# Moving the power tables of a state-space stage into PSUM, and reordering the stage

## The chip, the cores and the metric

The kernel runs on one core of a Trainium2 chip. The metric is device time in microseconds (us) for one launch; lower is better. Names of the engines: PE is TensorE (matmuls and transposes), DVE is VectorE, ACT is ScalarE, POOL is GpSimd, SP is SyncE, which here only issues DMAs.

## The reference

A block of eight stages on a sequence of 256 tokens of width 1024. The change touches the first stage only, a diagonal state-space mixer ("S5") with 64 groups of 16 channels and 64 complex states a group. Cut to what matters:

```python
def s5_mixer(x, a_re, a_im, log_dt, b_re, b_im, c_re, c_im, d_skip, w_glu, w_out):
    u = x.astype(f32).reshape(bsz, seq, SSM_GROUPS, SSM_GROUP)
    ...
    lbar_re = mag * jnp.cos(lam_im * dt)
    lbar_im = mag * jnp.sin(lam_im * dt)
    ...
    bu_re = jnp.einsum('blgh,gph->lbgp', u, bb_re)
    bu_im = jnp.einsum('blgh,gph->lbgp', u, bb_im)
    ...
    _, _, s_re, s_im = lax.associative_scan(
        _ssm_combine, (a_seq_re, a_seq_im, bu_re, bu_im), axis=0)
    y = (jnp.einsum('lbgp,ghp->blgh', s_re, c_re.astype(f32))
         - jnp.einsum('lbgp,ghp->blgh', s_im, c_im.astype(f32)))
    y = y.reshape(bsz, seq, D_MODEL) + d_skip.astype(f32) * x.astype(f32)
    h = jax.nn.gelu(y).astype(x.dtype)
    val, gate = jnp.split(h @ w_glu, 2, axis=-1)
    z = val * jax.nn.sigmoid(gate)
    return (z @ w_out).astype(x.dtype)
```

Seven stages of matmuls (gated feed-forwards, attention, a hybrid layer) follow. They are the same in both kernels.

## The kernel before

`s5_states` computes y and its gelu, `main_stream` all that follows. The tokens are cut into 32 blocks of 8. Inside a block the answer is a sum over lags; between blocks the states are carried by a tree over the 32 blocks. The 64 groups are handled in pairs: 32 pairs lie along the free axis, the 2 x 64 states of a pair on the 128 partitions.

The start (up to line 362) computes lambda and its powers `LR` = lambda^8 ... lambda^1 (real and imaginary part), and `LRs`, `LRd`, their sum and difference, in SBUF. A complex product is made of three real ones with these tables. The tables of B and C are transposed by PE to PSUM and copied by ACT to SBUF (`nBr`, `nBi`, `Cc`).

After that each piece of work is a named step, put on a fixed engine, and each engine runs its steps in the order of the string `ORDER`. The order of DVE, PE, ACT and POOL is thus written out by hand; only waits on data and on buffers move it. The steps, with lines, are these (the first digit is a part i, a half f or a channel tile ch):

- `cp`, `cs`: C times a coefficient (POOL, line 460) and its sums (DVE, lines 464 to 466).
- `vp`, `vt`, `vs`: 24 products B x power of 128x512 elements (DVE, line 470), four transposes of each (PE, line 500), the copy to SBUF (ACT, line 504). A product has six buffers, a transposed one two PSUM buffers (`pv`).
- `sm`, `sp`, `sd`, `st`, `ss`: block states by matmul (line 512), the copy of the shared third product (ACT, line 515), the sum (DVE, line 518), a transpose (line 524), the copy (ACT, line 535).
- `wp`, `wq`: 24 products C x power of 128x448 elements (POOL, line 470) and their sums (DVE for i = 0 to 5, POOL for 6 and 7; line 481).
- `bp`: powers of lambda for the tree (DVE, lines 542 to 551). `mg`, `bo`: the tree up and down for the halves f = 0 and 1 (DVE; each is a complex multiply-add of two products and two sums, lines 559 to 562).
- `lp`, `lc`, `lb`, `ld`, `lm`, `ls`: lag matrices (PE, line 606), their block diagonal (POOL at line 618, or ACT), the D term on lag 0 (POOL, lines 626 and 627), the matmuls over lags (PE, line 634, two PSUM buffers `py`), the copy out.
- `ms`, `om`, `os`, `ot`, `oa`, `og`, `oh`, `ol`: the states before each block, masked (ACT, line 588), times C (PE, line 653), copied, transposed (line 665), summed (line 669), gelu, and split in a high and a low half for the next stage.
- `wd`, `wh`, `wl`: the first weights of the next stage, loaded and split (line 705). Their raw buffer is one of four; loads of more weights wait on SP until one is free.

Line 470 stands for both DVE and POOL products, since both go through the helper `times`.

Of the kernel before, what the change touches and what calls it, by code (L numbers as in the profile page):

```python
# [166 lines left out]
vp71 xt10 cp10 bd01 cp11 xt01 xs10 vp10 vt71 cp00 cs1 ug1 vt10 wp61 vp72 ut1 wp01 vs10 cp01 vt72 wp21 vs71 vp42 vp12  # L167
us1 wp31 vp11 vt12 wp71 vp02 wp41 vs72 ut5 vt11 vp70 cs2 vp41 vs12 ut7 us5 vp00 vt70 vs11 vp50 wr1 sm1 vs70 wp11 wp72
vt00 vp32 us7 vp51 vt02 sp1 sm7 ug0 ut6 vs02 sd1 vp01 vs00 st1 vp52 vt50 ut2 us6 sp7 wp51 vs50 vt51 us2 vp31 vt52 vt32
vs51 bd00 vs52 ss1 sd7 wr0 wp12 ut0 vt01 vs01 vp61 sm5 vt31 cs0 vp30 st7 us0 ut4 sp5 dt xs01 ss7 sm0 vp22 sd5 wp52  # L170
wp42 vs32 vt22 vp40 vs31 vp21 vt40 ds wp40 wp00 wp30 bd11 vp20 vs22 wp22 us4 st5 vt30 xt00 sp0 bd10 wp32 vs30 xs00
wp02 sd0 ut3 st0 vt20 wq31 wq40 xt11 wq00 ss0 wp10 us3 sm3 vs20 wq01 wq10 ss5 wq11 vt21 vs21 wp20 vs40 lp1 wq21 vt61
wq41 sp3 bp0 xs11 sd3 sm2 st3 vt42 sp2 vp62 vs61 lp0 lb11 sd2 wp70 lc0 ss3 wq70 bp1 vp60 st2 lp4 vt62 vs42 ss2 lc4
wq20 vt60 wq71 lb10 vs60 lb00 mg00 ld1 lp7 mg01 lp2 lc2 vt41 lm1 vs62 sm6 lb40 bp2 ld0 mg02 vs41 ls1 sm4 ld4 lb20 sp6
bp3 wq30 bo00 sd6 wp50 lb70 sp4 lm0 lb71 sd4 lp3 lb31 ld2 st6 bo01 lm4 ls0 bo02 ss6 lb30 bo03 ls4 st4 ld7 lm7 ss4 ls7
wq51 bo04 bo05 wp62 ld3 ms01 wq50 ms00 mg10 mg11 wp60 lm3 wq60 lm2 wq61 lp6 lc6 mg12 wd lp5 lb51 ls2 lb60 lb50 bo10
bo11 ld5 om01 om00 bo12 ld6 os01 lm5 os00 bo13 ls3 ot1 bo14 bo15 ot3 lm6 ms11 oa1 ot2 ls5 oa3 om11 og1 ms10 oa2 og3
oh31 oh10 og2 wh1 os11 ol31 wh0 oh30 om10 ls6 oh21 ot0 ol10 oh20 ol21 oh11 os10 ol20 ol11 ol30 wl1 oa0 og0 ot4 wl0
oh00 ot6 oh01 oa4 og4 oa6 ot5 og6 ol01 ol00 ot7 oh41 ol41 oh61 ol61 oa7 oh60 oa5 og7 oh40 oh71 oh70 og5 ol40 ol60 ol70
ol71 oh51 oh50 ol51 ol50  # L180
# [3 lines left out]
def s5_states(nc, tc, a, V, S, G, T, const, raws, ats, mm_ps, tp_ps, xts, ident, h, **_):  # L184
    """y = SSM(x) + d * x, then gelu; returns the transposed halves [P, NK, SEQ] of it, and the next stage's
    first weights, split."""
# [26 lines left out]
    with tc.manual_schedule(engines=PAP):  # L213
# [111 lines left out]
        Cc = buf("c", [P, 2, NGP, SH])
        for k, raw in enumerate(c_raw):
            S.copy(Cc[:, k], transposed(lambda hh: raw[:, hh, :], py_ps))
        S.activation(out=sm([P, 1], "warm"), in_=Cc[:, 1, 0, 0:1], func=AF.Gelu_apprx_tanh)
# [208 lines left out]
        # states at the borders of the blocks, by a tree  # L537
        def border_power(lv):
            """lambda^(TC 2^lv)"""
            lr, li = sm([P, 2, NGP], f"Lr{lv}"), sm([P, 2, NGP], f"Li{lv}")  # L540
            if lv == 0:
                V.tensor_copy(lr[:, 0], LR[:, 0, 0, :])
                V.tensor_copy(li[:, 1], LR[:, 0, 1, :])
            else:
# [3 lines left out]
                V.tensor_sub(lr[:, 0], x1, d2)
                V.scalar_tensor_tensor(li[:, 1], pr, 2.0, pi, op0=ALU.mult, op1=ALU.mult)
            V.tensor_copy(lr[:, 1], lr[:, 0])  # L550
            V.tensor_scalar(li[:, 0], li[:, 1], -1.0, None, op0=ALU.mult)
            Lr.append(lr)
            Li.append(li)
# [977 lines left out]
```

## Time and profile before

| | us |
|---|---|
| median of 3 runs | 1397.32 |
| lowest and highest of them | 1396.32, 1399.21 |
| span of the profiled execution | 1397.1 |
| of it: from the start to the first matmul of the next stage | 114.0 |

Busy time over the whole span: PE 1353.8 us (97%), DVE 940.1 (67%), ACT 699.6 (50%), POOL 117.4 (8%). The profiled execution is the time from the first to the last instruction of one run. Shares over the whole span describe the seven matmul stages; the stage that the change touches is 8% of it, so it has to be read in windows of its own. In rows of the timeline the columns are start, duration, engine, line, operation, out<-in, shapes and count; merged rows give the duration of all their instructions together, and successive instructions of one engine overlap by some hundredths of a us.

### The profile page before, as it was taken

How to read it: one execution, taken by the hardware profiler on the slowest of the kernel's cores; microseconds unless marked ns; L12 is line 12 of the kernel's file. 1: busy time of each engine (PE TensorE's matmuls, PEld its weight loads, DVE VectorE, ACT ScalarE, POOL GpSimd, SP SyncE). 2: the span in 40 equal slices, each digit the busy share in tenths (PEclk: the TensorE clock that was granted, in tenths of full speed). 3: DMA queues.
4: the chain of work that ended last, by engine and by line, in shares of the span. 5: the costliest groups of instructions: out<-in, count | busy, mean ns of one | idle time of the engine just before them, and what ended most of it. 6: DMA issues, size and time to landing. Idle time of an engine off the chain costs nothing.

```text
span 1397.1 us, 20195 instructions
## 1 busy us (share of the span) xinstructions
PE 1353.8 (97%) x7192; PEld 1116.3 (80%) x7192; DVE 940.1 (67%) x1936; ACT 699.6 (50%) x1114; POOL 117.4 (8%) x178
## 2 busy tenths in 40 slices
PE   6879999999999999999999999999999999999998
PEld 5677878888788878888777888888888788888887
DVE  8896675555776875555788567564668956756463
ACT  3536544444577644444455545454554554545351
POOL 7650000000011100000110000000001000000000
PEclk8899999999999999999999999999999999999999
DMA  5005857555564366565455455564654545655561
GB/s 122 1 2 195 256 169 234 182 181 181 165 211 137 91 195 197 182 194 189 126 175 177 146 181 181 181 210 152 213 169 133 171 145 167 195 181 187 175 200 56
DMA packets 141285, 230.72 MB, mean 165 GB/s; under 512 B 15096, under 2 KB 83776, under 8 KB 141120
## 3 DMA queue, kind: packets, MB, share of 16 engines
q1 hardware_dynamic: 141184, 229.43, 52.3%
q8 instruction: 56, 0.92, 0.3%
q14 instruction: 45, 0.37, 0.1%
HBM read 228.35 MB, written 1.05 MB: 164 GB/s over the span
## 4 chain that ended last, share of the span: by engine, by line
PE 86%; DVE 8%; DMA 2%; issue 1%; ACT 1%; SPq 1%; POOL 0%; ACTq 0%; POOLq 0%; DVEq 0%
PE acc L807 8%; PE acc L808 8%; PE acc L806 8%; PE mm_ffn_g_t L807 6%; PE mm_ffn_g_t L808 6%; PE mm_ffn_g_t L806 6%; PE mm_ff_g_t L806 4%; PE mm_ff_g_t L808 4%; PE mm_ff_g_t L807 4%; PE tp L865 2%; PE mm_hy_t L806 2%; PE mm_hy_t L807 2%; PE mm_hy_t L808 2%; PE mm_hy_b_t L808 1%; PE mm_hy_b_t L806 1%
## 5 line engine op out<-in xcount | busy, mean ns | idle before, releaser
L769 DVE TENSOR_TENSOR wl<-raw,wh 128x512 fp32r<-128x512 f32 (+1 forms) x834 | 542.7, 684 | 159.8 <-ACT wh L763 143.7
L763 ACT CAST wh<-raw 128x1024 fp32r<-128x1024 f32 (+1 forms) x417 | 436.6, 1048 | 260.7 <-DMA raw<-in_ffn_w_gu_dram 41.1
L806 PE MATMUL acc<-wh,bTh 128*128 128x512 f32 x544 | 213.3, 392 | 0.0
L807 PE MATMUL acc<-wh,bTl 128*128 128x512 f32 x544 | 212.1, 390 | 0.5 <-DVE bTl L852 0.2
L808 PE MATMUL acc<-wl,bTh 128*128 128x512 f32 x544 | 212.1, 390 | 0.0
L806 PE MATMUL mm_ffn_g_t<-wh,xTh 128*128 128x512 f32 x352 | 141.2, 401 | 2.1 <-ACT xTh L851 2.1
L807 PE MATMUL mm_ffn_g_t<-wh,xTl 128*128 128x512 f32 x352 | 138.3, 393 | 0.5 <-DVE xTl L852 0.5
L808 PE MATMUL mm_ffn_g_t<-wl,xTh 128*128 128x512 f32 x352 | 138.0, 392 | 0.0
L852 DVE TENSOR_TENSOR bTl<-tp,bTh 128x256 fp32r<-128x256 f32 (+1 forms) x104 | 52.6, 512 | 122.8 <-ACT bTh L851 122.8
L807 PEld LDWEIGHTS acc<-wh,bTl 128*128 128x128 f32 x544 | 102.2, 188 | 22.6 <-DVE bTl L852 2.0
L808 PEld LDWEIGHTS acc<-wl,bTh 128*128 128x128 f32 x544 | 102.1, 188 | 21.3
L806 PEld LDWEIGHTS acc<-wh,bTh 128*128 128x128 f32 x544 | 102.1, 188 | 21.1 <-ACT bTh L851 0.3
L851 ACT CAST bTh<-tp 128x256 fp32r<-128x256 f32 (+1 forms) x104 | 45.2, 443 | 144.7 <-PE tp L865 131.0
L806 PE MATMUL mm_ff_g_t<-wh,xTh 128*128 128x512 f32 x256 | 102.6, 401 | 0.0
L808 PE MATMUL mm_ff_g_t<-wl,xTh 128*128 128x512 f32 x256 | 99.9, 390 | 0.0
L807 PE MATMUL mm_ff_g_t<-wh,xTl 128*128 128x512 f32 x256 | 99.7, 389 | 0.0
L806 PEld LDWEIGHTS mm_ffn_g_t<-wh,xTh 128*128 128x128 f32 x352 | 66.4, 189 | 15.2 <-ACT xTh L851 2.5
L808 PEld LDWEIGHTS mm_ffn_g_t<-wl,xTh 128*128 128x128 f32 x352 | 66.5, 189 | 14.0
L807 PEld LDWEIGHTS mm_ffn_g_t<-wh,xTl 128*128 128x128 f32 x352 | 66.6, 189 | 13.9 <-DVE xTl L852 1.1
L806 PE MATMUL mm_hy_t<-wh,xTh 128*128 128x512 f32 (+1 forms) x160 | 61.5, 384 | 1.2 <-DVE at L1312 0.6
L807 PE MATMUL mm_hy_t<-wh,xTl 128*128 128x512 f32 (+1 forms) x160 | 59.9, 374 | 1.5 <-DVE xTl L852 1.3
L808 PE MATMUL mm_hy_t<-wl,xTh 128*128 128x512 f32 (+1 forms) x160 | 59.9, 374 | 0.0
(458 smaller groups left out, 2137.9 us busy)
## 6 DMA issues: line engine op xcount, KB each, us to landing
raw<-in_w_ff_dram SPq DMA_DIRECT2D x128, 512.0 KB, 4.6
raw<-in_ffn_w_gu_dram SPq DMA_DIRECT2D x176, 256.0 KB, 4.2
raw<-in_w_in_dram SPq DMA_DIRECT2D x64, 512.0 KB, 4.4
raw<-in_ffn_w_down_dram SPq DMA_DIRECT2D x44, 512.0 KB, 4.9
raw<-in_ssm_w_glu_dram SPq DMA_DIRECT2D x32, 256.0 KB, 5.5
raw<-in_sb_w_qkv_dram SPq DMA_DIRECT2D x32, 256.0 KB, 4.3
raw<-in_w_out_dram SPq DMA_DIRECT2D x16, 512.0 KB, 4.5
raw<-in_ssm_w_out_dram SPq DMA_DIRECT2D x8, 512.0 KB, 4.7
```

What stands on the lines that cost most here:

```text
L763: S.copy(wh, raw)
L769: V.tensor_sub(l2[:, sl], r2[:, sl], h2[:, sl])
L806: T.matmul(ps, xh[:, k], wh, start=first, stop=False)
L807: T.matmul(ps, xl[:, k], wh, start=False, stop=False)
L808: T.matmul(ps, xh[:, k], wl, start=False, stop=last)
L851: S.copy(hi, ps)
L852: V.tensor_sub(lo, ps, hi)
L865: T.transpose(pt[:, k, :], src[:, k * P:(k + 1) * P], ident)
```

## The change

Tables in PSUM: two banks (`lt`), taken from the removed `py` buffers, hold lambda's sums, differences and negated real parts (`PRs`, `PRd`, `nPRr`) and, from ACT copies (`bt`), the tree's powers of levels 0 and 1. The products `vp`, `mg` and `bo` (levels 0 and 1) read them there. POOL's products keep tables in SBUF (`LRs`, `LRd`, now copied by ACT). C stays in PSUM, and its four products `cp` move from POOL to DVE. PE adds the third state product itself (a second matmul into the same accumulator), so that `sp` is gone and `sd` is a copy by ACT. The D term becomes a matmul with the identity into the lag matrices; `ld` is gone, and two small steps (`dk`, `dm`) prepare it. The signs of B and of a mask are swapped, which removes a negation on POOL. The order of the whole stage is new. `lm` now writes to the two `pv` buffers. Text changes of comments are left out here.

```diff
 ORDER = """
...
+ug1 cp10 cp11 cs1 bp0 xt00 xs00 vp10 cp01 wp01 cp00 ut1 bd11 ut5 wp61 wd vp11 vt10 wr1 us5 bt0 vp32 us1 ut3 wp21 vp12
+ug0 cs2 vp30 cs0 vt11 vs10 wp31 wp51 us3 vs11 xt01 vp31 dk vt12 ut2 vt30 xs01 vs12 wp22 wr0 vs30 vt31 wp02 vt32 vp20
+wp00 vp00 dt sm1 vp01 us2 ut4 bp1 wp20 bd00 vs31 vs32 ds sd1 us4 vt00 dm wp50 bd10 wp32 vs00 vp02 bd01 sm3 wq20 st1
+vp21 sd3 ut6 vt20 wq01 wp30 vt01 ut0 vs20 st3 vs01 ss1 us6 vt21 wp11 vp22 wq00 vt22 us0 xt10 ss3 vp51 vs21 lp0 vs22
+wq30 vp42 wp52 wh0 vt02 vs02 wq21 sm2 xs10 sm0 vp41 lc0 wp10 vt42 sd2 lp2 wq50 bt1 vt51 sd0 vp40 wq31 vs42 wp42 lc2
+vs51 vt40 vp61 vp62 lb00 st0 wp12 st2 ss0 vt41 wp40 vs40 vp52 bp2 wp71 wp72 ut7 lp3 vt52 vs41 lm0 sm4 ss2 wq51 lb31
+lb30 wp60 lb20 vs52 vp50 us7 ls0 wp70 wp62 sd4 vt50 wq10 wp41 vp71 vt61 wq11 lp1 vs50 vs61 st4 vp60 wq60 wq41 ss4 sm5
+vp70 lb10 lb11 lm3 ls3 vt60 vs60 vt62 xt11 mg00 vt70 vs62 lp5 mg01 sd5 vt71 wq61 vs70 lb50 st5 vs71 vp72 mg02 lm1 ss5
+bp3 bo00 lb51 wq40 xs11 vt72 sm6 vs72 bo01 bo02 lp4 sm7 bo03 ls1 wh1 sd7 sd6 lm5 lc4 st6 st7 lp6 bo04 lm2 bo05 ss6 ls5
+ss7 ms01 mg10 lb40 ms00 wq70 mg11 mg12 bo10 bo11 bo12 lm4 wq71 lp7 om01 lb70 ls4 ls2 om00 bo13 lb71 lm7 lc6 os01 bo14
+os00 ot1 ot0 bo15 lb60 ms11 ls7 lm6 oa1 oa0 ot2 oa2 og1 ms10 oh11 ol11 ls6 og0 om11 og2 oh01 om10 ot3 oh00 oh21 os11
+oh20 os10 ol01 wl1 wl0 ot6 oa3 oh10 og3 oh30 oh31 ol21 ol20 ol00 oa6 og6 ot4 ol10 oh61 ot5 oa4 og4 oh60 ol31 ot7 ol30
...
-    def py_ps(shape):
-        return zp.tile(shape, F32, name="py", tag="py")
+    lt = [zp.tile([P, 512], F32, name=f"lt{i}", tag=f"lt{i}", bufs=1) for i in range(2)]
...
-            S.mul(nb, transposed(lambda hh: raw[:, :, hh], py_ps), -1.0)
-        G.tensor_add(Bs, nBr, nBi)
-        G.tensor_scalar(Bs, Bs, -1.0, None, op0=ALU.mult)
...
+            S.copy(b, transposed(lambda hh: raw[:, :, hh], pv_ps))
+        G.tensor_add(Bs, Br, Bi)
+        Cc = [transposed(lambda hh: raw[:, hh, :], pv_ps) for raw in c_raw]
...
+        PRs, PRd, nPRr = (x.rearrange("p (t g) -> p t g", g=NGP) for x in (lt[0][:, :256], lt[0][:, 256:], lt[1][:, :256]))
+        V.tensor_add(PRs, LR[:, :, 0, :], LR[:, :, 1, :])
+        V.tensor_sub(PRd, LR[:, :, 0, :], LR[:, :, 1, :])
+        S.mul(nPRr, LR[:, :, 0, :], -1.0)
+        S.copy(LRs, PRs)
+        S.copy(LRd, PRd)
...
+        step("dk", lambda: V.tensor_reduce(mask16, ident.rearrange("p (g h) -> p h g", h=SH), axis=AX.X, op=ALU.add))
+        step("dm", lambda: G.tensor_mul(dmask, mask16.unsqueeze(1).to_broadcast([P, NK, SH]),
+                                        dsk.unsqueeze(2).to_broadcast([P, NK, SH])))
...
-            G.tensor_mul(w[:, k], Cc[:, i], coef[:, j, :].unsqueeze(2).to_broadcast([P, NGP, SH]))
+            V.tensor_mul(w[:, k], Cc[i], coef[:, j, :].unsqueeze(2).to_broadcast([P, NGP, SH]))
...
-            times(V, v, (Bs, nBi, nBr)[k], (LRr, LRs, LRd)[k], i, 0, TC)
+            times(V, v, (Bs, Bi, Br)[k], (nPRr, PRs, PRd)[k], i, 0, TC)
...
-                    T.matmul(ps[32 * q:32 * q + 32, :, cols], ug, vg, start=True, stop=True)
+                    out = ps[32 * q:32 * q + 32, :, cols]
+                    T.matmul(out, ug, vg[:, 1:3], start=True, stop=False)
+                    T.matmul(out, ug, vg[:, 0:1].to_broadcast([P, 2, 64]), start=False, stop=True)
...
-            V.tensor_add(tmp(("sls", i), "sls", [P, 2, P]), tl["ps", i][:, 1:3],
-                         tl["pa", i].unsqueeze(1).to_broadcast([P, 2, P]))
+            S.copy(tmp(("sls", i), "sls", [P, 2, P]), tl["ps", i])
...
+        def border_table(lv):
+            t = lt[1][:, 256 + 96 * lv:352 + 96 * lv].rearrange("p (i g) -> p i g", g=NGP)
+            S.copy(t, powers_at[lv])
+            powers_at[lv] = t
...
-            V.tensor_mul(m[0], x, Lr[lv][:, :, gs].unsqueeze(3).to_broadcast(shape))
-            V.tensor_mul(m[1], x[:, ::-1], Li[lv][:, :, gs].unsqueeze(3).to_broadcast(shape))
+            L = powers_at[lv]
+            V.tensor_mul(m[0], x, L[:, 0:1, gs].unsqueeze(3).to_broadcast(shape))
+            V.tensor_mul(m[1], x[:, ::-1], L[:, 1:, gs].unsqueeze(3).to_broadcast(shape))
...
+            T.matmul(ks[:, TC - 1], ident, dmask[:, ch], start=False, stop=True)
...
-        def lag_skip(ch):
-            k0 = tl["kb", ch].rearrange("p t g h -> p t (g h)")[:, TC - 1]
-            dg = tmp(("dg", ch), "pa", [P, P])
-            G.tensor_scalar(dg, ident, dsk[:, ch:ch + 1], None, op0=ALU.mult)
-            G.tensor_add(k0, k0, dg)
...
-            py = tl["py", ch] = py_ps([P, NC, TC])
+            py = tl["py", ch] = pv_ps([P, NC, TC])
```

## Rows read from the trace of the kernel before

**Rows 1.** Windows: start:end, length, PE, PEld, DVE, ACT, POOL busy, clock, DMA.
```profile
20.00:63.60 43.60, 35.43 (x316) 25.62 (x315) 39.10 (x50) 23.68 (x56) 32.58 (x25) 0.77 0.02 6
63.60:105.40 41.80, 33.48 (x400) 29.89 (x400) 40.81 (x87) 15.30 (x47) 25.30 (x25) 0.92 0.01 1
105.40:114.00 8.60, 7.89 (x161) 7.23 (x161) 4.95 (x15) 7.37 (x19) 0.00 (x0) 0.80 0.01 2
114.00:200.00 86.00, 81.73 (x373) 64.85 (x373) 61.54 (x117) 45.09 (x66) 3.02 (x18) 1.00 0.72 227
```

**Rows 2.** Chain that ended last, end of the stage: start, us, what.
```profile
104.69 0.70 DVE c L562
105.42 1.16 ACT big L588
106.62 5.44 PE mm L653 x128
```

**Rows 3.** Timeline of DVE, start of the stage and first products.
```profile
14.10 1.62 DVE L339 TENSOR_TENSOR mt<-LR 128x256 f32<-128x256 f32 x2
17.88 0.43 DVE L361 TENSOR_TENSOR LRs<-LR 128x256 f32<-128x256 f32 x1
18.55 0.68 DVE L470 TENSOR_TENSOR v<-nBi,LRs 128x512 f32<-128x512 f32 x1
25.22 1.48 DVE L470 TENSOR_TENSOR v<-nBr,LRd 128x512 f32<-128x512 f32 x1
36.37 0.41 DVE L518 TENSOR_TENSOR sls<-mm,pa 128x256 f32<-128x256 f32 x1
```

**Rows 4.** Timeline of POOL, the products beside the last of rows 3.
```profile
24.71 7.00 POOL L470 TENSOR_TENSOR big<-cc,LRs 128x448 f32<-128x448 f32 x5
34.47 4.22 POOL L470 TENSOR_TENSOR big<-cc,LRd 128x448 f32<-128x448 f32 x3
```

**Rows 5.** Groups by line and shape, 0 to 118 us, DVE: busy us, mean ns | idle before.
```profile
L470 DVE TENSOR_TENSOR v<-nBr,LRd 128x512 f32<-128x512 f32 x8 | 9.9, 1254 | 1.0 <-PE pv L500 1.0
L470 DVE TENSOR_TENSOR v<-Bs,LR 128x512 f32<-128x512 f32 x8 | 9.0, 1139 | 0.3 <-PE pv L500 0.3
L470 DVE TENSOR_TENSOR v<-nBi,LRs 128x512 f32<-128x512 f32 x8 | 8.8, 1104 | 1.5 <-PE pv L500 1.5
L481 DVE TENSOR_TENSOR big<-big,wa 128x448 f32<-128x448 f32 x12 | 8.7, 767 | 0.0
L518 DVE TENSOR_TENSOR sls<-mm,pa 128x256 f32<-128x256 f32 x8 | 3.2, 412 | 0.5 <-ACT pa L515 0.5
```

**Rows 6.** Timeline of DVE, powers and products of the tree.
```profile
56.95 1.10 DVE L542 COPY Lr<-LR 128x32 f32<-128x32 f32 x1
63.63 1.49 DVE L559 TENSOR_TENSOR mt<-c,Lr 128x512 f32<-128x512 f32 x1 [1.24 <-ACT c L535]
67.31 2.04 DVE L559 TENSOR_TENSOR mt<-sl,Lr 128x256 f32<-128x256 f32 x1
82.05 1.35 DVE L559 TENSOR_TENSOR mt<-c,Lr 128x256 f32<-128x256 f32 x1
92.40 2.04 DVE L559 TENSOR_TENSOR mt<-sl,Lr 128x256 f32<-128x256 f32 x1
```

**Rows 7.** Groups by line and shape, 0 to 118 us, POOL and ACT.
```profile
L626 POOL TENSOR_SCALAR pa<-ident,dsk 128x128 f32<-128x128 f32 x8 | 7.3, 913 | 0.1
L627 POOL TENSOR_TENSOR c<-c,pa 128x128 f32<-128x128 f32 x8 | 4.6, 570 | 2.1 <-issue 1.5
L535 ACT COPY c<-mm 128x256 f32<-128x256 f32 x8 | 3.1, 388 | 1.4 <-PE mm L524 1.4
L515 ACT COPY pa<-mm 128x128 f32<-128x128 f32 x8 | 2.2, 271 | 4.2 <-PE mm L512 3.0 <-POOL c L627 1.2
```

**Rows 8.** Timeline of PE: state matmuls, and output matmuls of one half.
```profile
46.78 0.88 PE L512 MATMUL mm<-vT,u 128*32 128x192 f32 x16
90.53 3.77 PE L653 MATMUL mm<-big,big 128*32 128x128 f32 x128
```

More of the change, by code (lines that the diff above doesn't have):

```diff
@@ L166 @@
 ORDER = """
[L167 to L180, printed above, removed]
+ug1 cp10 cp11 cs1 bp0 xt00 xs00 vp10 cp01 wp01 cp00 ut1 bd11 ut5 wp61 wd vp11 vt10 wr1 us5 bt0 vp32 us1 ut3 wp21 vp12
+ug0 cs2 vp30 cs0 vt11 vs10 wp31 wp51 us3 vs11 xt01 vp31 dk vt12 ut2 vt30 xs01 vs12 wp22 wr0 vs30 vt31 wp02 vt32 vp20
@@ L181 @@
+oa5 oh41 ol60 og5 oh40 oh51 oa7 ol41 og7 ol61 oh50 ol51 ol40 oh71 ol50 ol71 oh70 ol70
 """
@@ L319, in s5_states @@
         exp_poly(mag, -87.0)
-        nBr, nBi, Bs = (z.tile([P, NGP, SH], F32, name=n) for n in ("nBr", "nBi", "Bs"))
-        for nb, raw in zip((nBr, nBi), b_raw):
-            S.mul(nb, transposed(lambda hh: raw[:, :, hh], py_ps), -1.0)
-        G.tensor_add(Bs, nBr, nBi)
-        G.tensor_scalar(Bs, Bs, -1.0, None, op0=ALU.mult)
[L325 to L328, printed above, removed]
+        Br, Bi, Bs = (z.tile([P, NGP, SH], F32, name=n) for n in ("Br", "Bi", "Bs"))
+        for b, raw in zip((Br, Bi), b_raw):
+            S.copy(b, transposed(lambda hh: raw[:, :, hh], pv_ps))
+        G.tensor_add(Bs, Br, Bi)
+        Cc = [transposed(lambda hh: raw[:, hh, :], pv_ps) for raw in c_raw]
+        S.activation(out=sm([P, 1], "warm"), in_=Bi[:, 0, 0:1], func=AF.Gelu_apprx_tanh)
         dsk = sm([P, NK], "dsk")
@@ L360, in s5_states @@
         LRs, LRd = sm([P, TC, NGP], "LRs"), sm([P, TC, NGP], "LRd")
-        V.tensor_add(LRs, LR[:, :, 0, :], LR[:, :, 1, :])
-        V.tensor_sub(LRd, LR[:, :, 0, :], LR[:, :, 1, :])
-        xT, Lr, Li = [], [], []
+        PRs, PRd, nPRr = (x.rearrange("p (t g) -> p t g", g=NGP) for x in (lt[0][:, :256], lt[0][:, 256:], lt[1][:, :256]))
[4 more added lines that the diff above has]
+        S.copy(LRd, PRd)
+        squares, powers_at = [], []
         tl = {}
@@ L440, in s5_states @@
         step("ds", lambda: S.copy(dsk, tl["pd"]))
+        mask16, dmask = sm([P, SH], "mask16"), sm([P, NK, SH], "dmask")
+        step("dk", lambda: V.tensor_reduce(mask16, ident.rearrange("p (g h) -> p h g", h=SH), axis=AX.X, op=ALU.add))
+        step("dm", lambda: G.tensor_mul(dmask, mask16.unsqueeze(1).to_broadcast([P, NK, SH]),
+                                        dsk.unsqueeze(2).to_broadcast([P, NK, SH])))
         def input_block(k, e):
             bd = tmp(("bd", k), "bd", [P, NGP, 2, SH])
-            out, nb, m = bd[:, :, e, :], (nBr, nBi)[k], nmask2[:, e:e + 1]
+            out, nb, m = bd[:, :, e, :], (Br, Bi)[k], mask2[:, e:e + 1]
             if ON_POOL["bd"]:
@@ L506, in state_products @@
         def state_products(i):
-            ps = tl["ps", i] = mm_ps([P, 3, P])
+            ps = tl["ps", i] = mm_ps([P, 2, P])
             for q in range(4):
@@ L511, in state_products @@
                     ug, vg = u[i // 4][:, 2 * (4 * (i % 4) + q) + e, :], tl["vT", i][:, :, q, cols]
-                    T.matmul(ps[32 * q:32 * q + 32, :, cols], ug, vg, start=True, stop=True)
-        def state_part(i):
-            S.copy(tmp(("pa", i), "pa", [P, P]), tl["ps", i][:, 0])
+                    out = ps[32 * q:32 * q + 32, :, cols]
+                    T.matmul(out, ug, vg[:, 1:3], start=True, stop=False)
+                    T.matmul(out, ug, vg[:, 0:1].to_broadcast([P, 2, 64]), start=False, stop=True)
         def state_parts(i):
-            V.tensor_add(tmp(("sls", i), "sls", [P, 2, P]), tl["ps", i][:, 1:3],
-                         tl["pa", i].unsqueeze(1).to_broadcast([P, 2, P]))
+            S.copy(tmp(("sls", i), "sls", [P, 2, P]), tl["ps", i])
         def state_turn(i):
@@ L531, in s5_states @@
             step(f"sm{i}", state_products, i)
-            step(f"sp{i}", state_part, i)
             step(f"sd{i}", state_parts, i)
@@ L538, in border_power @@
         def border_power(lv):
-            lr, li = sm([P, 2, NGP], f"Lr{lv}"), sm([P, 2, NGP], f"Li{lv}")
+            L = sm([P, 3, NGP], f"L{lv}")
+            lr, li = L[:, 0], L[:, 2]
             if lv == 0:
-                V.tensor_copy(lr[:, 0], LR[:, 0, 0, :])
-                V.tensor_copy(li[:, 1], LR[:, 0, 1, :])
+                V.tensor_copy(L[:, 0::2], LR[:, 0])
             else:
-                pr, pi = Lr[-1][:, 0], Li[-1][:, 1]
+                pr, pi = squares[-1][:, 0], squares[-1][:, 2]
                 V.tensor_mul(x1, pr, pr)
                 V.tensor_mul(d2, pi, pi)
[L548 to L553, printed above, removed]
+                V.tensor_sub(lr, x1, d2)
+                V.scalar_tensor_tensor(li, pr, 2.0, pi, op0=ALU.mult, op1=ALU.mult)
+            V.tensor_scalar(L[:, 1], li, -1.0, None, op0=ALU.mult)
+            squares.append(L)
+            powers_at.append(L)
+        def border_table(lv):
+            t = lt[1][:, 256 + 96 * lv:352 + 96 * lv].rearrange("p (i g) -> p i g", g=NGP)
+            S.copy(t, powers_at[lv])
+            powers_at[lv] = t
         def cmac(dst, x, lv, f, n, plus):
@@ L583, in mask_states @@
         def mask_states(f, e):
-            src, m = before()[:, :, 16 * f:16 * f + 16, :], mask2[:, e:e + 1]
+            src, m = before()[:, :, 16 * f:16 * f + 16, :], nmask2[:, e:e + 1]
             if ON_POOL["sb"]:
@@ L591, in s5_states @@
             step(f"bp{lv}", border_power, lv)
+        for lv in range(2):
+            step(f"bt{lv}", border_table, lv)
         for f in range(2):
@@ L606, in lag_products @@
                     T.matmul(ks[32 * q:32 * q + 32], tl["bd", k][:, gp].rearrange("p e h -> p (e h)"), W(k)[:, gp],
-                             start=(k == 0), stop=(k == 1))
+                             start=(k == 0), stop=False)
+            T.matmul(ks[:, TC - 1], ident, dmask[:, ch], start=False, stop=True)
         def lag_copy(ch):
@@ L641, in s5_states @@
                 step(f"lb{ch}{part}", lag_blocks, ch, part)
-            step(f"ld{ch}", lag_skip, ch)
             step(f"lm{ch}", lags, ch)
```

## The prediction

> **What bounds the kernel now.** I read the windows first, because the shares of the whole span describe the stages that the change leaves alone. In the two windows from 20 to 105.4 us VectorE (DVE) is busy for 39.1 of 43.6 and for 40.8 of 41.8 us; TensorE (PE) is busy for 35.4 and 33.5 us of them, at granted clocks of 0.77 and 0.92, ScalarE (ACT) for 39.0 us together, GpSimd (POOL) for 57.9 [rows 1]. The chain of waits says the same of the end: the last product of the tree on DVE, then the mask on ACT, then the output matmuls on PE from 106.62 us [rows 2]. The next stage's first matmul comes at 114 us, and from then on PE is busy for 81.7 of 86 us [rows 1]. So what the first stage gains, the whole run gains: behind it stands a queue of PE work that starts earlier by as much. The two places to watch are therefore the time at which DVE ends the tree (105.4 us) and the time at which PE could start the output matmuls (106.6 us).
>
> Next I read DVE's timeline, because one kind of instruction has two prices there. A product of 512 elements takes 0.68 us at 18.55, where POOL stands still, and 1.48 at 25.22, where POOL multiplies too [rows 3], in five products of 1.40 us each [rows 4]. Both have their operands in SBUF, and they go in step. The row at 36.37 tells them apart: a sum of 256 elements with one operand in PSUM takes 0.41 us [rows 3] in the midst of three POOL products of 1.41 us [rows 4], no more than 256 elements from SBUF take while POOL is idle (0.43 at 17.88, [rows 3]). All eight such sums have a mean of 412 ns [rows 5]. So an operand in PSUM seems to free a DVE product from POOL.
>
> **The change part by part, on DVE.** All times are us against the profiled span of 1397.1, which is 0.2 below the median of the runs.
>
> *Products with the tables.* The 24 take 9.9 + 9.0 + 8.8 = 27.7 [rows 5]. With the table in PSUM each should cost what it costs alone, 0.68, so 16.3: a gain of 11.4.
>
> *Start of the stage.* From 14.10 to 17.88 the last four powers take 3.8 us [rows 3], beside POOL's products with C. These move to DVE, and start after the powers. Alone an instruction of 256 elements takes 0.43 or less, with overlap 0.34, so 1.4 for four: a gain of 2.4. The four products then cost DVE 4 x 0.68 = 2.7 and the mask sum `dk` at most another 0.3: a loss of 3.0.
>
> *State sums.* Eight sums of 3.2 in all leave DVE [rows 5]: a gain of 3.2.
>
> *Tree.* The first two products of levels 0 and 1 read PSUM: 16 products. Four of them took 1.49, 2.04, 1.35 and 2.04 [rows 6] where 0.68 (512) and 0.41 (256) is the price alone: 0.8 + 1.6 + 0.9 + 1.6 = 4.9, and a fifth is like the one of 1.35 and follows it; I take 5.5. The powers of the tree need 17 instructions instead of 22; two of them met POOL and took 1.1 each (one is shown, [rows 6]) for work of 0.2: a gain of 2.3.
>
> *Sums `wq`.* Here the new order costs something. Twelve sums of 448 elements take 8.7 now, 767 ns each [rows 5], since DVE does eight of them in a row while POOL waits for it. In the new order they stand one by one between the DVE products, while POOL works on its own, and they have both operands in SBUF. The bounds are the price alone, about 0.62 (a gain of 1.2), and POOL's step of 1.41 (a loss of 8.2). I take a loss of 4.5, half of them in step, because POOL will have more pauses than now: its 11.9 us for the D term are gone [rows 7].
>
> The sum: 11.4 + 2.4 - 3.0 + 3.2 + 5.5 + 2.3 - 4.5 = **17.3**. With the bounds of `wq` it is 13.6 to 23.0. DVE would end the tree at 105.4 - 17.3 = 88.1.
>
> [...]
>
> **On the other engines.** *PE* gets the state sum: 8 x 16 matmuls of 192 columns become 8 x 32 of 128. The first kind takes 0.88 for 16, the second by the output matmuls 3.77 / 4 = 0.94 for 32 [rows 8] at the full clock, 5.44 / 4 = 1.36 [rows 2] at a window's clock of 0.80 [rows 1]. So 0.5 to 3.8 in all, and I take 2. The D term adds 8 small matmuls, 0.5 at the price of these. PE has 35.4 + 33.5 = 68.9 of work between 20 and 105.4, which becomes 71.4 at the clocks of now. Scaled to the full clock it is 35.4 x 0.77 + 33.5 x 0.92 + 1 = 59. If PE never waited it could start the output matmuls at 79 (full clock) to 91.4 (clocks of now). DVE's 88.1 plus the mask of 1.2 lies inside: the two engines are now of one length, and PE is what is late next. I take DVE, because PE's clock is lowest where its work is thin (0.77 in the first window, with 81% busy), and the new order makes it denser.
>
> *ACT* loses eight copies of 271 ns and two of C, and gets eight of 388 ns [rows 7], three table copies and two small ones: about +1 on 39 of 85 us, hidden in its pauses. The copy `sd` waits for PE with the copies `vs` behind it, and PE's next transposes wait for those; but `sp`, which goes, had the same place and waited 4.2 in all [rows 7]. *POOL* loses 11.9 (D term), its products with C and a negation, and waits for nobody who is late. *The lag matmuls* now share two PSUM buffers with the transposes: a transpose may have to wait for a copy of about 0.39 [rows 7], up to eight times; I take nothing, the full price is 3. The load `wd` is named earlier in the order; the SP queue is idle there, and nothing stands behind it but loads that wait for a buffer anyway. At the end of the stage the splits of the first weights come a little earlier; up to 1 us, which I leave out.
>
> So 1397.1 - 17.3 = 1379.8, and **1380** for the median.
>
> **The rivals.** *PE takes over.* The order makes it dense, but its clock stays as now, and waits for buffers remain. Of PE's present pauses (85.4 - 68.9 = 16.5) half stay: 20 + 71.4 + 8 = 99.4 instead of 106.6, a gain of 7: 1390. For it: 59 us of full-clock work leave little room before 88. Against: its pauses now are mostly DVE's.
>
> *DVE goes freely.* POOL's pauses fall where `wq` stands, and the sums of the tree meet POOL less: gain 23 to 24: 1373.5.
>
> *PSUM does not free the products* (the change then doesn't do what it says). The row at 36.37 might have fallen into a gap between reads of POOL. Then the 11.4 and the 5.5 fall away, and C's products cost 1.48 instead of 0.68 each, 3.2 more: 17.3 - 20.1 = -2.8, so 1400, slower. Against it: eight sums, none of them slow.
>
> *PE's clock falls* (slower). With 59 us of full-clock work, PE alone reaches 106.6 if its mean clock from 20 us on is below 59 / 86.6 = 0.68; at 0.60 it takes 98 and the time is 1409. Against it: 0.77 and 0.92 now, with less work per us.
>
> **How the numbers follow.** The forecast, 1374 to 1386, has a chance of 0.58. PE takes over, about 1390: 0.20. DVE goes freely, about 1373.5: 0.13. PSUM does not free: 0.04. PE's clock falls: 0.03. The gains are given back behind the stage, no change: 0.02. A change of 0.2%, 2.8 us, is about what a measurement of this kernel can tell. So faster 0.91, same 0.02, slower 0.07. The range of 1372 to 1390 holds the forecast, the free DVE and half of PE's case, 0.81.
>
> **What would show it.** In the profile after, the 24 products take 0.68 each whether POOL works or not; if some take 1.4, the main term is wrong. The sums `wq` should be near 1.0 in the mean; at 0.6 or 1.4 that term was mis-sized. DVE should end the tree near 88, and the output matmuls should follow within 1.5 us; if PE starts them later than that, PE took over, and the clock of the windows from 20 us on says whether by its clock or by waits on `pv`. From the first matmul of the next stage to the end the run should last 1283 as now; if it is longer, the gain was given back. The forecast is wrong above all if PE is never idle from 20 us on.

## The result, and the profile after

The changed kernel takes 1380.15 us (median of four runs, 1378.03 to 1381.07); before, in the same series, 1397.92. The ratio is 0.9871, with a 95% interval of 0.9856 to 0.9885. The forecast was 1380. The number came true, but the picture behind it did not: VectorE (DVE) was to be the last to finish, and it is TensorE (PE).

Windows of the kernel after, with the columns of [rows 1]; the next stage's first matmul is at 97.24 us (before: 113.96).

```profile
20.00:63.60 43.60, 43.60 (x455) 38.08 (x453) 34.50 (x56) 27.45 (x71) 30.90 (x28) 1.00 0.02 5
63.60:85.00 21.40, 21.40 (x294) 19.71 (x295) 16.88 (x57) 11.30 (x32) 4.14 (x3) 1.00 0.01 2
85.00:97.24 12.24, 12.24 (x252) 11.52 (x242) 9.78 (x20) 6.55 (x19) 1.93 (x1) 1.00 0.01 3
```

Against [rows 1], PE and DVE have changed places. PE is busy for all of the 77.24 us, which the prediction had named as the sign of being wrong above all. Its clock stands at 1.00 instead of 0.77 and 0.92. That is the full clock only from 29.1 us on, where the first clock that the trace records begins; ahead of it the window prints 1.00, but the rows are slow. Eight transposes of one form, ahead of that point and behind it:

```profile
24.37 1.06 PE L409 MATMUL tp<-ident,xTh 32*128 32x32 f32 x8
35.07 0.68 PE L409 MATMUL tp<-ident,xTh 32*128 32x32 f32 x8
```

In the kernel before, eight of the same form take 1.06 at 41.26, where the granted clock is 0.50. (Its first record begins at 22.2 us, so the 0.77 of [rows 1] is a little too high as well: from there to 63.6 us it is 0.75.) DVE stands idle for 9.1 of the first 43.6 us, where it had 4.5 before. The chain of waits that ended last says the same: it stays on PE.

```profile
89.97 2.42 PE pv L639 x16
92.39 0.61 PE tp L669 x8
93.00 3.70 PE mm L657 x128
96.70 0.61 PE tp L669 x8
97.31 0.43 PE mm_s_g_t L810
```

In [rows 2] this chain came over from DVE and ACT to the output matmuls at 106.62. Now the same matmuls (line 657) follow PE's own work, and they cost 3.77 (from 92.93 on) instead of 5.44, with the clock full. The margin is small: the mask on ACT that they need too ends at 92.63, 0.30 us ahead of them.

```profile
91.48 1.15 ACT L596 ACTIVATE big<-c,mask 128x1024 f32<-128x1024 f32 x1 [4.21 <-DVE c L570]
```

The groups of DVE by line and shape (busy us, mean ns | idle before) are those of [rows 5], and below them the tree's product that took 2.04 us in [rows 6]:

```profile
L475 DVE TENSOR_TENSOR v<-Bi,lt 128x512 f32<-128x512 f32 x8 | 5.5, 683 | 0.8 <-PE pv L505 0.8
L475 DVE TENSOR_TENSOR v<-Br,lt 128x512 f32<-128x512 f32 x8 | 5.4, 682 | 4.0 <-PE pv L505 3.9
L475 DVE TENSOR_TENSOR v<-Bs,lt 128x512 f32<-128x512 f32 x8 | 5.4, 682 | 4.0 <-ACT lt L559 4.0
L486 DVE TENSOR_TENSOR big<-big,wa 128x448 f32<-128x448 f32 x12 | 10.4, 866 | 0.0
L567 DVE TENSOR_TENSOR mt<-sl,lt 128x256 f32<-128x256 f32 x2 | 0.8, 420 | 0.1
```

The 24 products with a table in PSUM take 16.3 us, 0.68 each, while POOL works beside them as before (30.9 of 43.6 us). That is the 11.4 us of the forecast to a tenth. The tree's product fell from 2.04 to 0.42. But the products now wait: mostly for PE, which is late in draining the transposes' input buffers, and once for a table copy. DVE's waits between 15 and 95 us (total us, times, longest):

```profile
DVE v L475 <- PE pv L505: 4.7, 5, 2.1
DVE v L475 <- ACT lt L559: 4.0, 1, 4.0
DVE mt L567 <- ACT c L537: 3.8, 1, 3.8
```

Behind these waits DVE finishes the tree at 91.44, not at 88.1:

```profile
90.75 0.69 DVE L570 TENSOR_TENSOR c<-mt,mt 128x512 f32<-128x512 f32 x1
```

PE's groups, 0 to 118 us, show what makes it the late one. Lines 518 and 519 are the state matmuls with the sum in PSUM, 618 the D term.

```profile
L518 PE MATMUL mm<-vT,u 128*32 128x128 f32 x128 | 16.0, 281 | 0.0
L519 PE MATMUL mm<-vT,u 128*32 128x128 f32 x128 | 15.8, 274 | 0.0
L618 PE MATMUL tp<-dmask,ident 128*128 128x16 f32 x16 | 3.2, 273 | 0.0
```

The two state groups run into each other, so that their times must not be added; read in the timeline from the start of a part to the next work, six parts take 2.3 to 2.7 us each (2.7 at the slow start) and two that follow each other directly 4.3 together: 18.9 in all, 2.36 in the mean. The forecast had 0.94 each.

### The profile page after: what moved, and what is told of

It is laid out like the page before. It is cut to its first block, busy times and chain, and to the rows that moved or that the text cites. A ratio compares the mean times of both kernels' runs of the same rounds, so it can differ in the third digit from the quotient of the medians.

```text
span 1376.1 us, 20457 instructions
## 1 busy us (share of the span) xinstructions
PE 1353.9 (98%) x7336; PEld 1124.1 (82%) x7336; DVE 918.5 (67%) x1928; ACT 700.2 (51%) x1117; POOL 93.5 (7%) x158
## 4 chain that ended last, share of the span: by engine, by line
PE 88%; DMA 5%; DVE 4%; ACT 1%; SPq 1%; issue 1%; POOL 0%; ACTq 0%; DVEq 0%; POOLq 0%
PE acc L811 8%; PE acc L812 8%; PE acc L810 8%; PE mm_ffn_g_t L811 6%; PE mm_ffn_g_t L812 5%; PE mm_ffn_g_t L810 5%; PE mm_ff_g_t L810 4%; PE mm_ff_g_t L812 4%; PE mm_ff_g_t L811 4%; PE tp L869 2%; PE mm_hy_t L811 2%; PE mm_hy_t L810 2%; PE mm_hy_t L812 2%; PE pv L639 1%; DMA raw<-in_ffn_w_gu_dram 1%; DMA raw<-in_ssm_w_glu_dram 1%
```

## The experiments

**The theories.** A: PE bounds the changed stage, because the state matmuls and the D term cost it far more than forecast; the tables in PSUM do free DVE. B: the state matmuls are slow by their nature (adding to the same words, a broadcast operand). C: DVE bounds, whatever PE does. D: the place of the tables does not matter, only the new order. Times are medians in us, ratios are to the kernel before, run beside each.

| kernel | time | ratio, 95% interval |
|---|---|---|
| c1, as changed | 1380.35 | 0.9876, 0.9857 to 0.9894 |
| e1, state matmuls interleaved | 1375.09 | 0.9838, 0.9823 to 0.9853 |
| e2, state sums on DVE | 1375.32 | 0.9848, 0.9829 to 0.9868 |
| e3, border table early | 1379.86 | 0.9875, 0.9860 to 0.9891 |
| e4, tables in SBUF | 1386.78 | 0.9927, 0.9911 to 0.9942 |
| e5, kernel before with tables in PSUM | 1389.33 | 0.9947, 0.9927 to 0.9967 |
| e6, without the D matmul | 1377.85 | 0.9862, 0.9846 to 0.9879 |
| e7, e1 and e3 together | 1375.33 | 0.9842, 0.9825 to 0.9859 |
| c2, e7 again | 1377.57 | 0.9849, 0.9829 to 0.9869 |
| e8, e7 with PE's pause filled | 1374.80 | 0.9833, 0.9818 to 0.9847 |
| e9, tables in SBUF, sums on DVE | 1393.07 | 0.9973, 0.9958 to 0.9987 |
| e10, state matmuls in another order | 1374.68 | 0.9844, 0.9826 to 0.9861 |

**c1, the changed kernel itself,** as the base of the first experiments.

> The changed kernel unaltered, beside the next three on one chip. Expected 1378 to 1381 by every theory; it is the yardstick for differences of a few us.

It repeats the result: 1380.35, with the next stage's first matmul at 98.46.

**e1, the state matmuls interleaved.** The same 256 matmuls, in the order group of the pair, part, quarter:

```diff
-            for q in range(4):
-                for e in range(G2):
+            for e in range(G2):
+                for part in range(2):
+                    for q in range(4):
```

> The 32 state matmuls of a part in another order: the four groups of 32 output partitions follow one another, instead of eight matmuls of one group in a row. Same matmuls, same sums. Theory A (PE bounds the changed stage, and the state sums cost 2.35 us a part instead of the predicted 0.94 because matmuls of one column group cannot overlap): about 1.0 us a part, 8 x 1.35 = 10.8 us less on PE, and 6 to 10 us less in all, 1370 to 1374, until DVE is late next. Theory B (the second matmul must wait for the first on the same PSUM columns, or the operand read with a repeat is slow): the parts stay at 2.2 to 2.4 us, 1378 to 1382.

Timeline of PE in e1: four of the eight parts of state matmuls, and the second half's output matmuls.

```profile
28.61 1.93 PE L520 MATMUL mm<-vT,u 128*32 128x128 f32 x32
40.16 1.96 PE L520 MATMUL mm<-vT,u 128*32 128x128 f32 x64
49.66 1.08 PE L520 MATMUL mm<-vT,u 128*32 128x128 f32 x32
89.31 5.38 PE L658 MATMUL mm<-big,big 128*32 128x128 f32 x128 [0.17 <-ACT big L597]
```

Two parts in 1.96 us are 0.98 each: the forecast's price, with the same adding and the same broadcast. B falls, but for one point: three other matmuls now stand between the two that add to the same words; e10 settles that. The run is 5.3 us shorter, so what bounded the stage was PE: A. It misses the 6 to 10 us expected. The eight parts take about 10 us instead of 18.9 (the first two 1.93 and 1.94, at the slow pace in which eight transposes take 1.06 at 30.47, against 0.68 at 34.84; the others about 1.0). Not all of that is gained, since DVE and the mask on ACT are late again (the row at 89.31 waits 0.17 for ACT), and that row takes 5.38 where the first half's output matmuls take 3.77 (at 77.12).

**e2, the state sums back on DVE.** The shared third product is copied by ACT and added by DVE, as before the change; all the rest stays.

```diff
-                    T.matmul(out, ug, vg[:, 1:3], start=True, stop=False)
-                    T.matmul(out, ug, vg[:, 0:1].to_broadcast([P, 2, 64]), start=False, stop=True)
+                    T.matmul(ps[32 * q:32 * q + 32, :, cols], ug, vg, start=True, stop=True)
...
-            S.copy(tmp(("sls", i), "sls", [P, 2, P]), tl["ps", i])
+            V.tensor_add(tmp(("sls", i), "sls", [P, 2, P]), tl["ps", i][:, 1:3],
+                         tl["pa", i].unsqueeze(1).to_broadcast([P, 2, P]))
```

> The state sums as before the change: one matmul of 192 columns, a copy by ACT, the sum by DVE; all else as changed, the copy and the sum where the copy by ACT stood. Theory A (PE bounds): a part costs about 0.85 us on PE, 8 x 1.5 = 12 us less; DVE gets 8 x 0.41 = 3.3 us more, hidden in its 12 us of waits: 6 to 10 us less, 1370 to 1374. Theory C (DVE bounds the stage, as the prediction took it): 3 us slower, 1383.

Faster by 5 us, a little less than expected, though DVE gets eight sums back. Taken alone, this part of the change, which the forecast booked as a gain of 3.2 on DVE and a loss of about 2 on PE, costs 5. C, by which it should have been slower, falls.

**e3, the border table early.** `bt1` stands right behind `bp1` in the order; DVE no longer waits 4 us for that copy.

> The copy of the tree's second power table is put right behind the power itself in the order, ahead of the ACT copies that wait for PE. In the changed kernel DVE waits 4.05 us for it at 39.4 us. Theory A (PE bounds): the wait is gone and the time stays, 1378 to 1381. Theory C (DVE bounds): 3 to 4 us less, 1376 to 1377.

The wait goes; those for PE are 10.9 us here, against 4.7 in the kernel after and 7.5 in c1:

```profile
DVE v L475 <- PE pv L505: 10.9, 6, 3.6
```

The time is unchanged within the interval: DVE's waits are not what the stage waits for. A.

**e4, the tables in SBUF,** the tree's too, with the new order, the state sums on PE and the D term kept:

```diff
-        PRs, PRd, nPRr = (x.rearrange("p (t g) -> p t g", g=NGP) for x in (lt[0][:, :256], lt[0][:, 256:], lt[1][:, :256]))
+        PRs, PRd, nPRr = LRs, LRd, sm([P, TC, NGP], "nPRr")
```

> The changed kernel with all its tables in SBUF again: the 24 products and the tree read the sums, differences, negated real parts and powers from SBUF, and the three start copies and two power copies by ACT are gone. C stays in PSUM. Theory A (an operand in PSUM frees DVE from POOL): the 24 products go from 0.68 to 1.1 to 1.3 us each, some 11 us more of DVE work; PE's length of 76 us hides part of it, DVE's waits of 12 us in the changed kernel the rest: 2 to 8 us slower, 1382 to 1388. Theory D (the place of the tables does not matter, the new order alone separates DVE and POOL): products stay near 0.7, 1378 to 1381.

DVE's groups in e4:

```profile
L483 DVE TENSOR_TENSOR big<-big,wa 128x448 f32<-128x448 f32 x12 | 12.3, 1023 | 0.0
L472 DVE TENSOR_TENSOR v<-Br,LRd 128x512 f32<-128x512 f32 x8 | 9.3, 1178 | 0.0
L472 DVE TENSOR_TENSOR v<-Bi,LRs 128x512 f32<-128x512 f32 x8 | 8.9, 1114 | 3.0 <-PE pv L502 3.0
L472 DVE TENSOR_TENSOR v<-Bs,nPRr 128x512 f32<-128x512 f32 x8 | 7.6, 960 | 0.0
```

The same products in the same order take 25.8 us instead of 16.3, and the run 6.4 more. D falls: it is the place of the table. A product takes 0.96 to 1.18 us in the mean with the table in SBUF, against 0.68 with the table in PSUM, and POOL works beside both (36.2 and 30.9 of the 43.6 us from 20 us on).

**e5, the kernel before with the 24 tables in PSUM,** in the old order. As in the change, their banks come from the lag matmuls, which now share the transposes' buffers; nothing else of it is taken over.

```diff
-            times(V, v, (Bs, nBi, nBr)[k], (LRr, LRs, LRd)[k], i, 0, TC)
+            times(V, v, (Bs, nBi, nBr)[k], (PRr, PRs, PRd)[k], i, 0, TC)
```

> The kernel before, in its old order, with one part of the change: the tables of the 24 products in PSUM (the banks taken from the lag matmuls, which use the transposes' two buffers). Theory A: the 24 products take 0.68 each, 11 us less DVE work, PE has no new work: 7 to 12 us faster than before, 1385 to 1390. Theory D: within 2 us of before, 1396 to 1399.

The products take 16.2 us here too, and the run 7.4 less than before: of the 11.4 us that DVE saves, a part is lost in waits of the old order (6 us for PE's `pv` at the products).

```profile
L473 DVE TENSOR_TENSOR v<-nBi,lt 128x512 f32<-128x512 f32 x8 | 5.5, 683 | 3.7 <-PE pv L503 2.9 <-ACT LRd L365 0.7
```

**e6, without the D matmul.** The D term is left out of the output.

```diff
-                             start=(k == 0), stop=False)
-            T.matmul(ks[:, TC - 1], ident, dmask[:, ch], start=False, stop=True)
+                             start=(k == 0), stop=(k == 1))
```

> The changed kernel without the eight matmuls of the D term (each takes 0.33 us on PE where 0.06 was predicted); the D term is left out of the output. Theory A (PE bounds, never idle): 2.6 us less, 1377 to 1378.5. Theory C (DVE bounds): no change, 1379.5 to 1381.

The time falls by 2.5 us, near what the rows of line 618 take (0.24 to 0.33 us from the start of a pair of the 16-column matmuls to the next work, 2.1 for the eight pairs), and in the profile the next stage's first matmul comes at 94.86 instead of 97.24. The intervals of e6 and c1 overlap, so this run alone would not decide; it fits A: what PE is spared, the run is spared.

**e7, e1 and e3 together,** and c2, the same kernel again.

> The interleaved state matmuls and the early power table together. With the matmuls interleaved PE is no longer late alone, and DVE ends the tree just ahead of the output matmuls. If DVE bounds then, its 4 us wait for the table now counts: 1371 to 1374. If PE still bounds: 1374 to 1376.

> The kernel of e7 once more, on the chip of e8, as the base of e8 and because the 3 us that its profile gained over e1's were not in its times. If the 3 us are real, 1372 to 1373; if the profile showed a quick execution, 1375 to 1375.5.

In both profiles the next stage starts earlier than in e1 (95.24), at 92.37 and 93.03, and yet the medians are not below e1's. All nine runs of this kernel lie between 1372.04 and 1379.59, wider than e1's five (1373.77 to 1376.27). The expectation of 1371 to 1374 was missed, and c2's 1377.57 lies above both of its own. A profile is of one execution: e1's is the longest of its five (1376.27), e7's the shortest of its four (1373.28). So a part of the earlier start may belong to the executions and not to the kernel; how much is not separated.

**e8, e7 with PE's pause filled.** In e1 and e7 PE stands idle 1.55 and 1.54 us shortly ahead of the second half's output matmuls, and these take 5.38 and 5.41 us instead of 3.77. Here PE repeats part of a lag step in that place:

```diff
+            for t in range(3 if ch == 6 else 0):
+                T.matmul(py[:, :, t:], kb[:, TC - 1 - t], xj[:, :, :TC - t], start=(t == 0), stop=(t == 2))
```

> As e7 (state matmuls interleaved, border table early), and PE repeats the first three lags of the last lag step (about 1.5 us of full-clock work) in the place where it stood idle 1.54 us ahead of the last transposes and output matmuls. The result is the same; the repeated products are written twice. Theory E, the clock fell to half because PE paused there: the second half's output matmuls take 3.8 instead of 5.4, the next stage's first matmul comes 1.6 to 2 earlier than in e7 (at about 90.6), and the time is 1.5 to 3 below e7's, 1372.3 to 1373.8. Theory F, the clock falls there for another reason: the output matmuls still take 5.4, and the time is e7's within 0.6, or up to 1 slower because the copy of the last lag step comes later.

The window from 86 to 92 us, first of e7, then of e8:

```profile
86.00:92.00 6.00, 5.83 (x137) 5.39 (x136) 2.59 (x6) 3.97 (x13) 0.00 (x0) 0.72 0.01 3
```

```profile
86.00:92.00 6.00, 5.82 (x153) 5.23 (x154) 3.90 (x10) 5.33 (x15) 0.00 (x0) 1.00 0.01 3
```

And the output matmuls of e8, with one of the next stage's matmuls:

```profile
86.86 3.77 PE L660 MATMUL mm<-big,big 128*32 128x128 f32 x128 [0.17 <-ACT big L597]
95.47 0.63 PE L815 MATMUL mm_s_g_t<-wl,xTh 128*128 128x512 f32 x1
```

With the pause filled (0.41 us of it are left) the granted clock is 1.00 instead of 0.72, the output matmuls take 3.77 instead of 5.41, and the next stage starts at 91.17, as theory E has it. But the pause alone does not make the clock fall. The kernel e4 has the same one (1.57), before the same work, and its output matmuls take 3.77 all the same; e7, then e4:

```profile
85.57 0.68 PE L670 MATMUL tp<-ident,u 32*128 32x32 f32 x8 [1.54 <-DVE raw L674]
86.42 5.41 PE L658 MATMUL mm<-big,big 128*32 128x128 f32 x128 [0.17 <-ACT big L597]
```

```profile
100.06 0.68 PE L664 MATMUL tp<-ident,u 32*128 32x32 f32 x8 [1.57 <-DVE raw L668]
100.91 3.77 PE L652 MATMUL mm<-big,big 128*32 128x128 f32 x128 [0.17 <-ACT big L591]
```

In e1, c2 and e10 the output matmuls are as slow as in e7 (5.38 to 5.44 us). So theory E is not shown by one execution of e8. Its time of 1374.80 missed the expected 1372.3 to 1373.8, and cannot be told from e7's. Behind the stage a stretch of slow matmuls (0.63 us instead of 0.40) is left, which e7 has too; the granted clock in the first 25 us of the next stage is 0.93 in both. The profiled execution of e8 spends 1281.7 us behind the next stage's first matmul, that of e7 1279.0, and most of the difference lies 400 us and more after it (in the 400 us from there PE does 1914 matmuls instead of 1924), where the two programs are the same. From 800 us behind that matmul to the end the granted clock is 0.99 in e8 and 1.00 in e7. A gain of 1 us in the stage is below that scatter.

**e9, tables in SBUF and sums on DVE:** the edits of e4 and e2 together, so the new order, the D term and C's products on DVE nearly alone.

> The new order and the D term on PE, but power tables in SBUF (as e4) and state sums on ACT and DVE (as e2): the new order nearly alone. In e4 the tables in SBUF made DVE late again, and PE had pauses (40.3 of 43.6 busy). Theory A (what counts is the longer of two engines): with DVE the longer one, the sums cost DVE 3.2 there and PE's saving of some 11 is worth nothing: 1388 to 1391, slower than e4 by 1 to 4. Theory C2 (PE is late in e4 too): faster than e4 by 2 to 5, 1382 to 1385. Between the first matmul of the next stage and the end 1279 to 1280, as in all kernels with the new order; 1282 to 1283 as in the old order would say that this part does not belong to the order.

Slower than e4 by 6.3, where A had 1 to 4. DVE waits for the copy of the third product as well as adding it:

```profile
DVE sls L520 <- ACT pa L517: 7.5, 4, 2.2
```

The profiled execution was this kernel's longest (1397.32), so its other numbers are not used; from the next stage's first matmul to the end it takes 1282.1, not the 1279 to 1280 expected, at a granted clock of 0.99 in the last 482 us, as in e8. Together with e2, e4 and c1 it makes a square:

| | sums on DVE | sums on PE, as written |
|---|---|---|
| tables in SBUF | 1393.07 | 1386.78 |
| tables in PSUM | 1375.32 | 1380.35 |

The same edit gains 6.3 where DVE is late and costs 5.0 where PE is. The tables are worth 17.8 while PE has room and 6.4 when it has none. The order, the D term and C's products on DVE bring 3.7. Not all of the 6.3 and the 17.8 is DVE's work: PE's clock is lower in e9, too. The mean granted clock of its ten runs is 0.986 to 0.993, that of e4's six 0.996 to 1.000 and of e2's four 0.994 to 0.998. How much the clock has of either number is not separated.

**e10, groups change earlier.** Only the two outer loops of the state matmuls are exchanged; the two matmuls into the same words still follow each other.

```diff
-            for q in range(4):
-                for e in range(G2):
+            for e in range(G2):
+                for q in range(4):
```

> The changed kernel with only the two loops of the state matmuls exchanged (group of a pair outside, quarter q inside): the two matmuls into the same words still follow each other, but PE goes on to another quarter of 32 output partitions after 4 instructions instead of 8. It tells why the interleaved order of e1 took 0.98 per part instead of 2.35. Theory G, matmuls to one quarter in a row do not overlap: the price falls with the length of the row, to 1.2 to 1.7 per part, and the time to 1375 to 1378. Theory W, the second matmul waits for the first because it adds to the same words: the price stays at 2.2 to 2.5 per part, and the time at 1380 within 1.

Timeline of PE, one part of the state matmuls: the kernel after (four of its rows), then e10 (all four).

```profile
32.31 0.41 PE L518 MATMUL mm<-vT,u 128*32 128x128 f32 x2
32.55 0.38 PE L519 MATMUL mm<-vT,u 128*32 128x128 f32 x2
32.77 0.41 PE L518 MATMUL mm<-vT,u 128*32 128x128 f32 x4
32.99 0.41 PE L519 MATMUL mm<-vT,u 128*32 128x128 f32 x4
```

```profile
31.05 0.45 PE L518 MATMUL mm<-vT,u 128*32 128x128 f32 x8
31.29 0.42 PE L519 MATMUL mm<-vT,u 128*32 128x128 f32 x8
31.51 0.44 PE L518 MATMUL mm<-vT,u 128*32 128x128 f32 x8
31.73 0.44 PE L519 MATMUL mm<-vT,u 128*32 128x128 f32 x8
```

One instruction takes 0.27 us in both. In e10 eight of them go in 0.45 us, two for each of the four quarters; in the kernel after at most four, so two quarters beside each other, and at either end of the part only one. A part takes 1.0 to 1.1 instead of 2.4, even less than the 1.2 to 1.7 expected of G. W falls. The kernel takes 1374.68, a little below the 1375 to 1378 of G, and all its runs (1373.94 to 1375.97) lie below all of c1's (from 1377.49): with this exchange of two lines it beats both kernels. The number of instructions in a row also fits the rows of before: there both the state matmuls and the output matmuls change the quarter after four ([rows 8]: 0.88 for 16, 3.77 for 128). That e10 comes out level with e2 says that the place of the state sums decides little once they are cheap on PE: DVE is then last again, with the tree done at 85.78 and the output matmuls from 87.01 on, in 5.44 us.

## Why the prediction was right, and where not

*Products with the tables, 11.4.* Right to a tenth, both in the kernel after (27.7 to 16.3) and alone (e5). With the table in PSUM one takes 0.68 us, as one from SBUF does alone [rows 3].

*Start of the stage, a gain of 2.4 and a loss of 3.0.* Right: the last four powers take 1.3 us instead of 3.8, C's products 2.6 and the mask sum 0.4.

*Tree, 5.5.* Right for the 16 products that read PSUM: they now take 9.5 us instead of 15.2, a gain of 5.7. The tree's other 48 instructions, which the forecast left out, fell from 23.1 to 18.8 as well.

*Sums `wq`, a loss of 4.5.* Too large: 8.7 became 10.4, a loss of 1.7. Between the 0.62 alone (at 65.30, with POOL idle) and POOL's step of 1.41 a mean of 866 ns is a third in step, not half: POOL is busy for 37 us of the stage instead of 58. In e4, with the same order, they take 1023 ns.

*Powers of the tree, a gain of 2.3.* Wrong in sign: six of the new instructions take 743 ns in the mean for work of 0.2, and the sum is 6.9 instead of 6.4. They too have both operands in SBUF: two of them take 1.02 (at 26.55) and 1.84 us (at 48.95) while POOL multiplies, and 0.18 and 0.19 (at 64.54 and 64.76) while it is idle.

*DVE as a whole, 17.3.* From 20 us to the end of the tree DVE works 57.7 us instead of 79.9, so 22.2 less. The rival "DVE goes freely" was nearer to its work than the forecast, mostly by those 48 instructions. DVE could not use it, as some 12 us of waits came in.

*State matmuls, 0.5 to 3.8.* This is the step that failed. The price of 0.94 for 32 was read off the output matmuls, which go on to another quarter of the output partitions after four instructions; the state matmuls as written do so after eight. They take 2.36 in the mean, so 18.9 instead of 7.0 for the eight parts at the full clock (0.88 each, [rows 8]): 11.9 more, three times the upper bound. The rows of [rows 8] were of the right kind and size, but not of the right order, and the bound should have asked which other partitions the next matmul goes to.

*D term, 0.5.* Mis-sized: 2.1 by the rows, 2.5 by e6. An instruction of 16 columns takes 273 ns, as one of 128 does (281 at line 518); the forecast had scaled it down.

*PE in all.* With these two terms the prediction's own sum comes near: 58 us of old work at the full clock, 11.9 and 2.1, make 72.0; PE takes 72.9 from 20 us to the output matmuls at 92.93. That it comes so near is in part luck. The 9.1 us ahead of 29.1 went at the slow pace; at the later one they would take an estimated 5.6 to 5.8 (by the transposes above, 0.61 to 0.68 against 0.99 to 1.06), so that PE would need some 69.5 us at the full clock, and 2 to 3 too much stand in the sum. The rival "PE takes over" thus happened, with more work than it had and without the pauses it assumed and, from 29.1 us on, without the low clock. That the clock would rise with denser work was the argument for DVE and against the slow rival. The shares of [rows 1] do not carry it: PE is busy for 81% at 0.77, for 80% at 0.92 and for 92% at 0.80. The trace of before does in part: behind pauses of PE of 2.37 us (ahead of 59.64) and 3.59 us (ahead of 77.02) the granted clock is 0.50, from 60 to 62.5 and from 77.5 to 80 us. In the kernel after it is 1.00 from 29.1 us to the output matmuls, without a pause; that the denser work is what raised it is not shown.

*Why the number came true all the same.* Two errors met. DVE shed 5 us more work than forecast, and PE got some 13 more, but nearly all at the full clock; so the output matmuls start at 92.93 rather than at 89.3, and then the lower clock that they had before (0.80 in [rows 1]) is gone (3.77 instead of 5.44), and the next stage starts 4.3 behind instead of 7.3. That the two errors cancelled is luck. The stage became 16.7 us shorter, the median 17.8.

*Given back later.* No. From the next stage's first matmul to the end the profiled executions take 1278.9 instead of 1283.1. That is no gain of the change to this amount: the profiled execution of before (1399.21 as timed) lay 1.3 above its median and that of after 2.1 below, and before has two stretches of 3.4 us at the half clock there, at 500 and 701 us, where after has none beyond 105 us. In the first 50 us of the next stage PE does the same work in both (146 of its first matmuls against 148, and 18 transposes of the first stage more), so nothing was given back there either, and nothing gained.

*The shared buffers `pv`, 0 to 3,* show no wait of PE: its only wait between 15 and 98 us is one of 3.6 us for a DMA at the start.

## What to carry to other kernels

In this stage a VectorE product beside GpSimd was priced by where its operands lay: one of them in PSUM took it from 1.15 us in the mean to 0.68, and the run was 17.8 us shorter with the tables there where PE had room (e2 against e9; not all of it is DVE's work) and 6.4 where it had none (c1 against e4). Before work is moved to the engine next in line, add up that engine's work at its full clock with the moved work, and take the price from instructions in the same order, not only of the same shape; the same move gained 6 us or cost 5, depending on which engine was late (and with it on PE's clock). Try small matmuls into 32 output partitions in an order that goes round the four quarters: here 32 of them took 1.0 to 1.1 us with the quarter changing after four instructions, and 2.36 with it changing after eight.

## What the runs showed of the hardware

Matmuls into 32 output partitions, one quarter of them, followed each other at 0.11 us (four rows of the kernel after start at 69.83, 69.94, 70.05 and 70.16, each of 0.27), and those into other quarters ran beside them, as long as the quarter changed soon enough: where it changed after four instructions all four ran together (e10: eight instructions in 0.45 us, 1.0 to 1.1 for 32), where it changed after eight only two (at most four instructions in 0.41, 2.36 for 32 in the mean). That eight in a row halve it was not expected, and what in PE makes it so is not shown.

Behind an idle stretch of PE of 1.54 or 1.55 us the output matmuls took 5.38 to 5.44 us in e1, e7, c2 and e10 (granted clock 0.72 from 86 to 92 us in e7), and with most of it filled (e8) 3.77, at 1.00; but behind one of 1.57 us in e4 they took 3.77 too. In e1, e3, e6, e7, e8 and the kernel after, a stretch of about 3 us or more with 0.63 us a matmul instead of 0.40 follows in the next stage (in the kernel after from 101.5 us on, with a granted clock of 0.50 from 101 to 104 us), though PE had no pause right ahead of it; c1 and c2, the same kernels as after and e7, show none (up to 105.9 and 109.8 us). What decides it is open.

A product of DVE waited 4.05 us for ACT's copy of the border table, though it reads other columns of the same bank. That the chip would need the two in this order is not shown.

```profile
43.49 0.69 DVE L475 TENSOR_TENSOR v<-Bs,lt 128x512 f32<-128x512 f32 x1 [4.05 <-ACT lt L559]
```
